# Attention scores of several heads issued in turns into one two-bank PSUM tile, value sums in two other banks

## The chip, the cores and the metric

The kernel runs on one core of a Trainium2 chip. The metric is the device time of one execution in microseconds (us), as the median of several runs. The engines are named as the profile names them: PE (TensorE, matmul), PEld (its weight loads), DVE (VectorE), ACT (ScalarE), POOL (GpSimd) and SP (SyncE, which issues the DMA transfers).

## The reference: two layers of a hybrid decoder

The input is one sequence of 256 tokens of width 1024. Each of two layers adds half a gated feed-forward block, a mixer and another half feed-forward block:

```python
for l in range(DEPTH):
    x = x + 0.5 * swiglu(rms_norm(x, norm_gain[l, 0]), w_ffn_in[l, 0], w_ffn_out[l, 0])
    x = x + hybrid_mixer(rms_norm(x, norm_gain[l, 1]), ...)
    x = x + 0.5 * swiglu(rms_norm(x, norm_gain[l, 2]), w_ffn_in[l, 1], w_ffn_out[l, 1])
```

The mixer projects its input into the queries, keys and values of four attention branches of four heads each: A (keys picked by an indexer, one shared key and value head), B (block-sparse), C (latent, with heads of 96 columns) and D (dilated, three groups of four heads, mixed by their softmax denominators). Each branch's output is projected, multiplied by a sigmoid gate, and summed over branches:

```python
branches = jnp.stack([o.reshape(b, t_len, BRANCH_WIDTH) for o in (out_a, out_b, out_c, out_d)], axis=2)
gates = jax.nn.sigmoid(gate_logits.reshape(b, t_len, N_BRANCH, D_MODEL) + b_gate)
merged = jnp.einsum('btnc,ncd->btnd', branches, w_branch)
return jnp.sum(gates * merged, axis=2) @ w_out
```

The output has the shape of the input, in float32.

## The kernel before

Tokens are handled in two tiles of 128 (`i` = 0, 1). The large products (feed-forward, projections, gates, output) run on operands that are split into a high and a low part: ACT casts a weight tile to `whi` (L187), DVE subtracts to get `wlo` (L188), and `mm3` issues three matmuls (L192 to L194). One such split serves 8 to 24 matmuls.

In the mixer the projections come first, then the attention of a branch stands beside the gates and the merge (output projection) of an earlier branch. `ORD` is B, C, A, D: the program writes the attention of B and C, then the gates and merge of B, the attention of A, gates and merge of C, the attention of D, gates and merge of A, and at last gates and merge of D. A scheduler then sets the order on each engine by priority and its own forecast of times, so that matmuls of gates and merges stand between those of the attention.

The attention of one branch and token tile (`att_tile`) loops over four heads. For each head the scores are one f32 matmul of 128 queries by n = 128 (i+1) keys (L791), for D three of them (L808 for i = 0, L817 for i = 1), one for each group. The profile shows one f32 matmul as two PE instructions. Heads of A, B and D have 64 columns, and two heads stand above each other on the partitions: even heads on rows 0 to 63, odd heads on rows 64 to 127, so that such a matmul uses one half of PE's rows. Heads of C take 96 rows. Then `softmax_pv` follows: DVE adds the bias and takes the row maximum (`tensor_tensor_reduce`, L551, called a read of the scores below), for D and i = 1 in two pieces; DVE negates it (`nm`, L557); ACT takes the exponential (L559); PE transposes the result (L567), DVE or ACT copies it (L571, L569), and PE multiplies it by the values (L574) into the tile `ov`. After four heads `finish` divides by the sums (L579, L581), transposes (L588) and splits the result (L590, L591). For A the bias is made by POOL from the indexer's choice (L799).

Eight PSUM banks are in use: two each for `pm` and `pt`, and four with the tags a0 to a3 for the rest. A score tile (`sl`) takes one bank, in turn a0, a1, a2; `ov` always takes a3:

```python
def s_tile():
    turn[0] += 1
    return pa.tile([128, 512], F32, name="sl", tag=f"a{turn[0] % 3}")[:]
```

A tile's place is given to the next tile of the same tag when all that read or wrote it have ended. The feed-forward's four sums (`acc`), the projections' pairs (`zp`) and the output's pairs (`xo`) use the same four banks.

Of the kernel before, what the change touches and what calls it, by code (L numbers as in the profile page):

```python
# [9 lines left out]
F32 = mybir.dt.float32  # L10
F32R = mybir.dt.float32r
AF = mybir.ActivationFunctionType
ALU = mybir.AluOpType
# [5 lines left out]
NT = 2  # L19
# [3 lines left out]
NFF = DFF // 128  # L23
# [4 lines left out]
CUT = -3e38  # L28
# [40 lines left out]
def tile_trunk(ctx: ExitStack, tc: tile.TileContext, a: dict, out: bass.AP):  # L69
# [145 lines left out]
    def ffn(l, s, nxt=None, aside=None):  # L215
# [86 lines left out]
        def grow(i):  # L302
            for h in range(2):
                xs = x[:, i, h * 512:(h + 1) * 512]
                nc.vector.scalar_tensor_tensor(out=xs, in0=acc[2 * i + h][:], scalar=0.5, in1=xs,
                                               op0=ALU.mult, op1=ALU.add)
                if nxt is None:
                    nc.sync.dma_start(out=out[0, i * 128:(i + 1) * 128, h * 512:(h + 1) * 512], in_=xs)
# [7 lines left out]
        def down(m, w, i):  # L316
            wh, wl = w
            ah, al = act[m]
            for h in range(2):
                t = slice(i * 128, (i + 1) * 128)  # L320
                n = slice(h * 512, (h + 1) * 512)
                mm3(acc[2 * i + h][:], ah[:, t], al[:, t], wh[:, 0, n], wl[:, 0, n], m == 0, m == NFF - 1)

        w0, todo = first(0)
        w1, more = first(1)
# [1 line left out]
        hh, hl, rs, rb, rows = yield todo  # L327
        yield from up_first(0, w0)
        rows()
        acc = [pa.tile([128, 512], F32, name=f"acc{j}", tag=f"a{j}") for j in range(4)]  # L330
        for j in range(1, NFF // 2):
            if j < 2:
                for _ in up_first(j, w1):
# [116 lines left out]
    def mixer(l, nxt):  # L450
# [6 lines left out]
            return gT[:, c:c + 1]  # L457

        def tiles():
            turn[0] += 2  # L460
            return [pa.tile([128, 512], F32, name="zp", tag=f"a{(turn[0] + i) % 4}") for i in range(NT)]

        def weights(c0, n, slots=own, pool=()):
            for q in range(2):
# [72 lines left out]

        brh, brl = {}, {}

        def softmax_pv(i, logits, pv, o, h):  # L540


            mx = sm.tile([128, 16], F32, name="mx", tag="mx")
            e = wk.tile([128, 768], F32, name="e", tag="e", bufs=3)
            off = 0
            for j, (ps, b) in enumerate(logits):
                n = int(np.prod(ps.shape[1:]))
                ev = e[:, off:off + n]
                if len(ps.shape) == 3:
                    ev = ev.rearrange("p (g s) -> p g s", g=ps.shape[1])  # L550
                nc.vector.tensor_tensor_reduce(out=ev, in0=ps, in1=b, scale=1.0, scalar=CUT, op0=ALU.add,  # L551
                                               op1=ALU.max, accum_out=mx[:, j:j + 1])
                off += n
            nm = sm.tile([128, 16], F32, name="nm", tag="nm")
            if len(logits) == 2:
# [37 lines left out]
        def pair(t, h):  # L593
            return t[64 * (h % 2):64 * (h % 2) + 64, h // 2, :]
# [191 lines left out]

        def plain(q_of, k_of, v, vh, bias_of):
            def one(i, h, o):
                n = 128 * (i + 1)
                ps = s_tile()  # L790
                nc.tensor.matmul(ps[:, :n], lhsT=q_of(h)[:, i * 128:(i + 1) * 128], rhs=k_of(h)[:, :n],  # L791
                                 start=True, stop=True)
                softmax_pv(i, [(ps[:, :n], bias_of(i, h)[:, :n])], lambda j: v[:, j, vh(h), :], o, h)
            return one

        def bias_a(i, h):
            n = 128 * (i + 1)
# [4 lines left out]
        def one_d(i, h, o):  # L802
            n = 128 * (i + 1)
            qs = slice(i * 128, (i + 1) * 128)
            if i == 0:
                ps = s_tile().rearrange("p (g s) -> p g s", g=4)
                for g in range(3):
                    nc.tensor.matmul(ps[:, g, :], lhsT=pair(dq, 4 * g + h)[:, qs], rhs=pair(dk, 4 * g + h)[:, :n],  # L808
                                     start=True, stop=True)
                bv4 = bias[:, 8:20, :].rearrange("p (g h) s -> p g h s", h=4)  # L810
                lg = [(ps[:, 0:3, :], bv4[:, :, h, 128:])]
            else:
                p0 = s_tile().rearrange("p (g s) -> p g s", g=2)
                p1 = s_tile()
                for g in range(3):
                    d = p0[:, g, :] if g < 2 else p1[:, :256]
                    nc.tensor.matmul(d, lhsT=pair(dq, 4 * g + h)[:, qs], rhs=pair(dk, 4 * g + h)[:, :n],  # L817
                                     start=True, stop=True)
                bv4 = bias[:, 8:20, :].rearrange("p (g h) s -> p g h s", h=4)
                lg = [(p0, bv4[:, 0:2, h, :]), (p1[:, :256], bias[:, 16 + h, :])]  # L820
            nb = i + 1
            softmax_pv(i, lg, lambda j: dv[:, j % nb, 4 * (j // nb) + h, :], o, h)

        one_a = plain(lambda h: pair(aq, h), lambda h: ak[64 * (h % 2):64 * (h % 2) + 64, 0, :], av,
                      lambda h: 0, bias_a)
# [1 line left out]
                      lambda i, h: bias[:, 4 + h, 256 - 128 * (i + 1):])  # L827
        one_c = plain(lambda h: cq[:, h, :], lambda h: ck[:, h, :], cv, lambda h: h,
                      lambda i, h: bias[:, 20, 256 - 128 * (i + 1):])


        yts = [wk.tile([128, 4, T], F32, name="yt", tag="xn") for _ in range(2)]
# [50 lines left out]
        for j, n in enumerate(ORD):  # L883
            for m in ORD[j + (j > 0):j + 2]:
                for i in range(NT):
                    att_tile(m, i, ones[m])
# [9 lines left out]
        def out_part(ps, i, h, e):  # L896
            t = slice(i * 128, (i + 1) * 128)
            wh, wl = w[4 * h + e]
            for k in range(2):
                kk = 2 * e + k  # L900
                mm3(ps[:], yh[kk // 4][:, kk % 4, t], yl[kk // 4][:, kk % 4, t], wh[:, k, :], wl[:, k, :],
                    kk == 0, kk == KC - 1)

        def add(ps, i, h):
            xs = x[:, i, h * 512:(h + 1) * 512]
            nc.vector.tensor_tensor(xs, ps[:], xs, op=ALU.add)

        ps = [[pa.tile([128, 512], F32, name="xo", tag=f"a{2 * h + i}") for i in range(NT)] for h in range(2)]
# [73 lines left out]
```

## Time and profile before

| | us |
|---|---|
| median of three runs | 1406.47 |
| the runs | 1399.9, 1406.47, 1406.78 |
| the profiled execution, its time | 1401.21 |
| its span, first to last instruction | 1399.4 |
| PE busy in the span | 1373.0 (98%) |
| DVE busy | 881.5 (63%) |
| ACT busy | 679.1 (49%) |
| POOL busy | 258.5 (18%) |

The profile page gives busy times of the engines, the chain of work that ended last, and the costliest groups of instructions; views of the trace list instructions in order of time with start, duration and the idle time before them. [...] The two layers stand in the trace at about 0 to 700 us and 700 to 1400 us; the attention of the first runs from 314 to 452 us, that of the second from 1003 to 1142 us.

### The profile page before, as it was taken

The numbers are of one execution on the slowest core, as the hardware profiler recorded it, in microseconds if no ns is written. First come the engines' busy times: TensorE is split into PE (matmuls) and PEld (weight loads), VectorE is DVE, ScalarE is ACT, GpSimd is POOL, SyncE is SP. The second block draws the span as 40 slices with busy tenths as digits, with TensorE's granted clock in tenths as the row PEclk, the third lists the DMA queues.
The fourth block names the chain that finished last, engine by engine and source line by source line (L and its number), as shares of the span: only waits on it lengthen the run. The fifth ranks groups of instructions, "written<-read, shape, count | busy, mean of one in ns | idle before, by whom it ended". The sixth has DMA issues, their size and how long they took to land.

```text
span 1399.4 us, 23259 instructions
## 1 busy us (share of the span) xinstructions
PE 1373.0 (98%) x9393; PEld 1262.6 (90%) x9393; DVE 881.5 (63%) x1498; ACT 679.1 (49%) x1052; POOL 258.5 (18%) x209
## 2 busy tenths in 40 slices
PE   7999999999999999999999999999999999999998
PEld 7998989879988989999999999898899989899997
DVE  6536556786696686555475555567866866765552
ACT  6425434655444556444454444355554454554441
POOL 0101132130022041111301111322200312211110
PEclk9999999999999999999999999999999999999999
DMA  9549634554442366555555555354534424665530
GB/s 353 171 158 374 239 118 127 186 167 151 127 145 77 135 206 208 189 181 181 181 170 192 181 181 196 95 185 145 188 121 148 133 70 145 214 208 193 188 121 31
DMA packets 173597, 237.10 MB, mean 169 GB/s; under 512 B 5085, under 2 KB 144545, under 8 KB 173489
## 3 DMA queue, kind: packets, MB, share of 16 engines
q1 hardware_dynamic: 172275, 235.16, 50.7%
q8 instruction: 74, 1.21, 0.3%
q10 hardware_dynamic: 1182, 0.38, 0.1%
q14 instruction: 34, 0.28, 0.1%
q0 software_dynamic: 32, 0.07, 0.0%
HBM read 234.51 MB, written 5.21 MB: 171 GB/s over the span
## 4 chain that ended last, share of the span: by engine, by line
PE 93%; DVE 3%; ACT 2%; DMA 1%; issue 1%; SPq 0%; ACTq 0%; DVEq 0%; POOLq 0%
PE pm L194 17%; PE pm L193 17%; PE pm L192 17%; PE acc L192 6%; PE acc L193 6%; PE acc L194 6%; PE zp L193 4%; PE zp L194 4%; PE zp L192 4%; PE ov L574 2%; PE sl L791 1%; DVE wlo L188 1%; PE pt L567 1%; PE xo L194 1%; PE xo L193 1%; PE sl L817 1%
## 5 line engine op out<-in xcount | busy, mean ns | idle before, releaser
L187 ACT CAST whi<-raw 128x1024 fp32r<-128x1024 f32 (+5 forms) x446 | 451.8, 1020 | 478.9 <-PE pm L193 293.1
L188 DVE TENSOR_TENSOR wlo<-raw,whi 128x1024 fp32r<-128x1024 f32 (+3 forms) x426 | 515.4, 1215 | 265.9 <-ACT whi L187 258.6
L192 PE MATMUL pm<-hh,whi 128*128 128x256 f32 x1664 | 473.8, 285 | 4.5 <-DVE tg L872 2.7
L194 PE MATMUL pm<-hh,wlo 128*128 128x256 f32 x1664 | 474.3, 285 | 0.8 <-DVE wlo L188 0.8
L193 PE MATMUL pm<-hl,whi 128*128 128x256 f32 x1664 | 473.1, 284 | 0.0
L192 PEld LDWEIGHTS pm<-hh,whi 128*128 128x128 f32 x1664 | 317.9, 191 | 9.1 <-ACT whi L187 5.0
L194 PEld LDWEIGHTS pm<-hh,wlo 128*128 128x128 f32 x1664 | 317.9, 191 | 4.7 <-issue 2.7
L193 PEld LDWEIGHTS pm<-hl,whi 128*128 128x128 f32 x1664 | 318.0, 191 | 4.4 <-issue 2.0
L296 POOL TENSOR_TENSOR act<-av,act 128x256 fp32r<-128x256 f32 x72 | 96.0, 1334 | 545.0 <-ACT act L295 540.6
L193 PE MATMUL acc<-wlo,act 128*128 128x512 f32 x352 | 138.2, 393 | 0.0
L192 PE MATMUL acc<-whi,act 128*128 128x512 f32 x352 | 138.2, 394 | 0.0
L194 PE MATMUL acc<-whi,act 128*128 128x512 f32 x352 | 137.9, 392 | 0.0
L193 PE MATMUL zp<-wlo,hh 128*128 128x512 f32 (+4 forms) x320 | 115.6, 362 | 0.2
L194 PE MATMUL zp<-whi,hl 128*128 128x512 f32 (+4 forms) x320 | 114.4, 359 | 0.0
L192 PE MATMUL zp<-whi,hh 128*128 128x512 f32 (+4 forms) x320 | 106.7, 359 | 0.0
L288 DVE TENSOR_TENSOR z<-pm,rb 128x512 f32<-128x512 f32 x72 | 49.7, 691 | 56.7 <-PE pm L194 56.5
L194 PEld LDWEIGHTS acc<-whi,act 128*128 128x128 f32 x352 | 66.1, 188 | 15.0
L192 PEld LDWEIGHTS acc<-whi,act 128*128 128x128 f32 x352 | 66.1, 188 | 13.3
L193 PEld LDWEIGHTS acc<-wlo,act 128*128 128x128 f32 x352 | 66.2, 188 | 13.1
L874 POOL TENSOR_TENSOR yt<-yt,tg 128x512 f32<-128x512 f32 x24 | 37.9, 1599 | 213.7 <-DVE tg L872 205.1
L194 PE MATMUL pm<-whi,hl 128*128 128x256 f32 x256 | 72.9, 285 | 2.6 <-DVE hl L139 2.6
L192 PE MATMUL pm<-whi,hh 128*128 128x256 f32 x256 | 73.0, 285 | 0.7 <-ACT hh L136 0.7
(191 smaller groups left out, 1794.2 us busy)
## 6 DMA issues: line engine op xcount, KB each, us to landing
raw<-in_w_ffn_in_dram SPq DMA_DIRECT2D x66, 1024.0 KB
raw<-in_w_in_dram SPq DMA_DIRECT2D x52, 1024.0 KB
raw<-in_w_ffn_out_dram SPq DMA_DIRECT2D x44, 1024.0 KB
raw<-in_w_ffn_in_dram SPq DMA_DIRECT2D x44, 512.0 KB
raw<-in_w_branch_dram SPq DMA_DIRECT2D x8, 1024.0 KB
raw<-in_w_out_dram SPq DMA_DIRECT2D x8, 1024.0 KB
raw<-in_w_in_dram SPq DMA_DIRECT2D x8, 768.0 KB
rep<-ld SPq DMA_DIRECT2D x1, 4032.0 KB
```

Of the source, the lines that this page charges most:

```text
L187: nc.scalar.copy(hv, src)
L188: (eng or nc.vector).tensor_tensor(lv, src, f(hv), op=ALU.subtract)
L192: nc.tensor.matmul(ps, lhsT=lh, rhs=rh, start=start, stop=False)
L193: nc.tensor.matmul(ps, lhsT=lh, rhs=rl, start=False, stop=False)
L194: nc.tensor.matmul(ps, lhsT=ll, rhs=rh, start=False, stop=stop)
L288: nc.vector.tensor_tensor(z[:], ps[:], rb[:].rearrange("p (o t) -> p o t", o=1) .to_broadcast([128, 2, T]), op=ALU.mult)
L296: nc.gpsimd.tensor_tensor(al, av[:], f(ah), op=ALU.subtract)
L567: nc.tensor.transpose(ps[:, c, :], p[:, (done + c) * 128:(done + c + 1) * 128], ident[:])
L574: nc.tensor.matmul(o[:, h, :], lhsT=pT[:, j, :], rhs=pv(j), start=j == 0, stop=j == nb - 1)
L791: nc.tensor.matmul(ps[:, :n], lhsT=q_of(h)[:, i * 128:(i + 1) * 128], rhs=k_of(h)[:, :n], start=True, stop=True)
L817: nc.tensor.matmul(d, lhsT=pair(dq, 4 * g + h)[:, qs], rhs=pair(dk, 4 * g + h)[:, :n], start=True, stop=True)
L874: nc.gpsimd.tensor_tensor(y, y, t[:], op=ALU.add)
```

## The change

- Scores get a tile of two banks with one tag, a01 (`s_pair`). For A, B and C the four heads of a token tile are issued one after the other, heads 0 and 2 into the first bank, 1 and 3 into the second (n columns each, at column 0 or 256). All four matmuls are written ahead of the four reads.
- For D two heads go together. For i = 0 the three groups are issued in turns (group 0 of both heads, group 1 of both, group 2 of both), one bank for each head. For i = 1 the first two groups of both heads fill one pair of banks, and group 2 of both takes a second pair.
- Two heads of a token tile share one tile `e` of exponentials where they fit (`logits_tiles`), with a maximum column of their own.
- `ov` alternates between a2 and a3.
- The feed-forward's first two sums, every second pair of projections and the first pair of the output become one tile of the tag a01 too; a2 and a3 stay single.

No instruction is added or taken away; what changes is their order and which tile a matmul waits for.

```diff
-        def s_tile():
+        def s_pair():
+
+            p = pa.tile([128, 2, 512], F32, name="sl", tag="a01")
+            return p[:, 0, :], p[:, 1, :]
+
+        def att_tile(n, i, scores, pv, together):
+
+
             turn[0] += 1
-            return pa.tile([128, 512], F32, name="sl", tag=f"a{turn[0] % 3}")[:]
-
-        def att_tile(n, i, one):
-            o = pa.tile([128, 4, 65], F32, name="ov", tag="a3")
-            for h in range(4):
-                one(i, h, o)
+            o = pa.tile([128, 4, 65], F32, name="ov", tag=f"a{2 + turn[0] % 2}")
+            for h0 in range(0, 4, together):
+                hs = range(h0, h0 + together)
+                for h, lg in zip(hs, scores(i, hs)):
+                    softmax_pv(i, lg, pv(i, h), o, h)
             finish(n, i, o)
...
+                two = s_pair()
+                ps = [two[h % 2][:, 256 * (h // 2):256 * (h // 2) + n] for h in hs]
+                for p, h in zip(ps, hs):
+                    nc.tensor.matmul(p, lhsT=q_of(h)[:, i * 128:(i + 1) * 128], rhs=k_of(h)[:, :n],
+                                     start=True, stop=True)
+                es = logits_tiles(2, n) + logits_tiles(2, n)
+                return [logits_sum(e, p, bias_of(i, h)[:, :n]) for e, p, h in zip(es, ps, hs)]
...
+            if i == 0:
+                ps = [p.rearrange("p (g s) -> p g s", g=4) for p in s_pair()]
                 for g in range(3):
...
+                    for p, h in zip(ps, hs):
+                        product(p[:, g, :], g, h)
...
+            ps = [p.rearrange("p (g s) -> p g s", g=2) for p in s_pair()]
+            for g in range(2):
+                for p, h in zip(ps, hs):
+                    product(p[:, g, :], g, h)
+            es = logits_tiles(1, 768) + logits_tiles(1, 768)
+            es = [logits_sum(e, p, bv4[:, 0:2, h, :]) for e, p, h in zip(es, ps, hs)]
+            ps = s_pair()
+            for p, h in zip(ps, hs):
+                product(p[:, :256], 2, h)
...
+        acc01 = pa.tile([128, 2, 512], F32, name="acc01", tag="a01")
+        acc = [acc01[:, 0, :], acc01[:, 1, :]]
...
+            turn[0] += 1
+            if turn[0] % 2:
+                return [pa.tile([128, 512], F32, name="zp", tag=f"a{2 + i}")[:] for i in range(NT)]
+            z = pa.tile([128, 2, 512], F32, name="zp", tag="a01")
+            return [z[:, 0, :], z[:, 1, :]]
```

**PE where the attention of D begins, first layer, before.** `sl` are scores, `pt<-ident,e` transposes of exponentials, `ov` value sums (`av_a` of branch A), `x3` three equal matmuls in a row.

```order
L567 MATMUL pt<-ident,e 128x128 x2
L808 MATMUL sl<-dk,dq 128x128 x6
L567 MATMUL pt<-ident,e 128x128 x2
L574 MATMUL ov<-av_a,pT 128x65 x2
L567 MATMUL pt<-ident,e 128x128 x2
L808 MATMUL sl<-dk,dq 128x128 x3
L574 MATMUL ov<-av_a,pT 128x65 x2
L808 MATMUL sl<-dk,dq 128x128 x3
L567 MATMUL pt<-ident,e 128x128 x2
L574 MATMUL ov<-av_a,pT 128x65 x2
L817 MATMUL sl<-dk,dq 128x256 x3
```

The same place after the change; `pm` are matmuls of gates.

```order
L830 MATMUL sl<-dk,dq 128x128 x4
L586 MATMUL ov<-av_a,pT 128x65 x2
L579 MATMUL pt<-ident,e 128x128 x2
L830 MATMUL sl<-dk,dq 128x128 x2
L192 MATMUL pm<-hh,whi 128x256
L193 MATMUL pm<-hl,whi 128x256
L194 MATMUL pm<-hh,wlo 128x256
L586 MATMUL ov<-av_a,pT 128x65 x2
L579 MATMUL pt<-ident,e 128x128 x2
L586 MATMUL ov<-av_a,pT 128x65 x2
L830 MATMUL sl<-dk,dq 128x128 x6
L586 MATMUL ov<-av_a,pT 128x65 x2
```

Before, the six scores in one row are three of head 0 and then three of head 1, and heads 2 and 3 follow alone. After, the rows of four, two and six alternate between an even and an odd head, and the next row of scores (four of 128x256, for i = 1) stands directly behind the last one above.

**DVE at the same place, before.** `ISA e,mx<-sl` is a read of scores, `ISA mx` its maximum.

```order
L571 COPY pT<-pt 128x256
L551 ISA e,mx<-sl,ba 128x256
L551 ISA mx 128x1
L188 TENSOR_TENSOR wlo<-raw,whi 128x1024
L557 TENSOR_SCALAR nm<-mx 128x1
L551 ISA e,mx<-sl,bias 128x384
L551 ISA mx 128x1
L571 COPY pT<-pt 128x256
L551 ISA e,mx<-sl,bias 128x384
L551 ISA mx 128x1
L557 TENSOR_SCALAR nm<-mx 128x1 x2
```

DVE after the change.

```order
L583 COPY pT<-pt 128x256
L558 ISA e,mx<-sl,bias 128x384
L558 ISA mx 128x1
L558 ISA e,mx<-sl,bias 128x384
L558 ISA mx 128x1
L881 TENSOR_TENSOR tg<-pm,rb 128x512
L569 TENSOR_SCALAR nm<-mx 128x1 x2
L188 TENSOR_TENSOR wlo<-raw,whi 128x1024
L558 ISA e,mx<-sl,bias 128x384
L558 ISA mx 128x1
L558 ISA e,mx<-sl,bias 128x384
L558 ISA mx 128x1
```

The reads of D's heads now come in twos, and a gate's scaling (L881) and a `wlo` stand between the reads of heads 0 and 1 and those of heads 2 and 3.

## Rows read from the trace of the kernel before

**Rows 1.** The profile page: span, busy time of engines, chain that ended last.

```profile
span 1399.4 us, 23259 instructions
PE 1373.0 (98%) x9393; PEld 1262.6 (90%) x9393; DVE 881.5 (63%) x1498; ACT 679.1 (49%) x1052; POOL 258.5 (18%) x209
PE 93%; DVE 3%; ACT 2%; DMA 1%; issue 1%; SPq 0%; ACTq 0%; DVEq 0%; POOLq 0%
```

**Rows 2.** PE in order of time, a lone 128-column score: start, duration, line, names, count.

```profile
319.79 0.28 PE L192 MATMUL pm<-hh,whi 128*128 128x256 f32 x1
320.00 0.48 PE L791 MATMUL sl<-bqk 64*128 64x128 f32 x2
320.42 0.39 PE L193 MATMUL pm<-hl,whi 128*128 128x256 f32 x1
320.64 0.28 PE L194 MATMUL pm<-hh,wlo 128*128 128x256 f32 x1
320.76 0.27 PE L192 MATMUL pm<-hh,whi 128*128 128x256 f32 x1
```

**Rows 3.** PE in order of time: one 128-column score of branch C.

```profile
332.29 0.37 PE L193 MATMUL pm<-hl,whi 128*128 128x256 f32 x1
332.49 0.38 PE L791 MATMUL sl<-ck,cq 96*128 96x128 f32 x2
332.63 0.36 PE L194 MATMUL pm<-hh,wlo 128*128 128x256 f32 x1
332.83 0.28 PE L192 MATMUL pm<-hh,whi 128*128 128x256 f32 x1
```

**Rows 4.** PE in order of time: a lone 256-column score; then a row of two.

```profile
411.56 0.28 PE L193 MATMUL pm<-hl,whi 128*128 128x256 f32 x1
411.77 0.70 PE L791 MATMUL sl<-aqk 64*128 64x256 f32 x2
412.39 0.39 PE L194 MATMUL pm<-hh,wlo 128*128 128x256 f32 x1
412.62 0.28 PE L192 MATMUL pm<-hh,whi 128*128 128x256 f32 x1
...
325.53 0.28 PE L194 MATMUL pm<-hh,wlo 128*128 128x256 f32 x1
325.74 0.70 PE L791 MATMUL sl<-bqk 64*128 64x256 f32 x4
326.37 0.39 PE L192 MATMUL pm<-hh,whi 128*128 128x256 f32 x1
326.59 0.28 PE L193 MATMUL pm<-hl,whi 128*128 128x256 f32 x1
```

**Rows 5.** PE in order of time: scores of branch D.

```profile
429.37 1.26 PE L808 MATMUL sl<-dk,dq 64*128 64x128 f32 x12
431.55 0.93 PE L808 MATMUL sl<-dk,dq 64*128 64x128 f32 x6
434.62 1.56 PE L817 MATMUL sl<-dk,dq 64*128 64x256 f32 x6
449.29 1.13 PE L817 MATMUL sl<-dk,dq 64*128 64x256 f32 x4
```

**Rows 6.** DVE and PE in order of time where D begins.

```profile
430.54 1.22 DVE L188 TENSOR_TENSOR wlo<-raw,whi 128x1024 fp32r<-128x1024 f32 x1
431.68 0.15 DVE L557 TENSOR_SCALAR nm<-mx 128x1 f32<-128x1 f32 x1
431.74 0.55 DVE L551 CUSTOM_DVE_ANT_1 e<-sl,bias 128x384 f32<-128x384 f32 x1
432.21 0.42 DVE L571 COPY pT<-pt 128x256 f32<-128x256 f32 x1
...
429.26 0.69 DVE L849 TENSOR_TENSOR tg<-pm,rb 128x512 f32<-128x512 f32 x1 [0.23 <-PE pm L194]
437.51 0.44 PE L588 MATMUL pt<-ident,bo 128*128 128x128 f32 x2 [0.73 <-DVE bo L581]
```

**Rows 7.** Busy us (and instructions) by stretch; then granted clock, DMA share and rate.

```profile
385.00:420.00 35.00, 33.67 (x248) 30.07 (x247) 31.35 (x88) 16.41 (x28) 9.05 (x8) 1.00 0.45 143
420.00:455.00 35.00, 34.12 (x242) 29.29 (x241) 23.61 (x67) 16.31 (x28) 7.98 (x9) 1.00 0.24 79
1110.00:1145.00 35.00, 34.11 (x243) 29.29 (x242) 23.61 (x68) 16.23 (x27) 8.42 (x8) 1.00 0.26 85
```

More of the change, by code (lines that the diff above doesn't have):

```diff
@@ L304, in grow @@
                 xs = x[:, i, h * 512:(h + 1) * 512]
-                nc.vector.scalar_tensor_tensor(out=xs, in0=acc[2 * i + h][:], scalar=0.5, in1=xs,
+                nc.vector.scalar_tensor_tensor(out=xs, in0=acc[2 * i + h], scalar=0.5, in1=xs,
                                                op0=ALU.mult, op1=ALU.add)
@@ L329, in ffn @@
         rows()
-        acc = [pa.tile([128, 512], F32, name=f"acc{j}", tag=f"a{j}") for j in range(4)]
+        acc01 = pa.tile([128, 2, 512], F32, name="acc01", tag="a01")
+        acc = [acc01[:, 0, :], acc01[:, 1, :]]
+        acc += [pa.tile([128, 512], F32, name=f"acc{j}", tag=f"a{j}")[:] for j in (2, 3)]
         for j in range(1, NFF // 2):
@@ L538, in mixer, with logits_tiles, logits_sum @@
         brh, brl = {}, {}
-        def softmax_pv(i, logits, pv, o, h):
[L543 to L553, printed above, removed]
+        def logits_tiles(n, ncol):
+            e = wk.tile([128, 768], F32, name="e", tag="e", bufs=3)
+            return [(e[:, j * ncol:(j + 1) * ncol], 0, sm.tile([128, 16], F32, name="mx", tag="mx"), 0)
+                    for j in range(n)]
+        def logits_sum(e, ps, b):
+            ev, off, mx, j = e
+            n = int(np.prod(ps.shape[1:]))
+            out = ev[:, off:off + n]
+            if len(ps.shape) == 3:
+                out = out.rearrange("p (g s) -> p g s", g=ps.shape[1])
+            nc.vector.tensor_tensor_reduce(out=out, in0=ps, in1=b, scale=1.0, scalar=CUT, op0=ALU.add,
+                                           op1=ALU.max, accum_out=mx[:, j:j + 1])
+            return ev, off + n, mx, j + 1
+        def softmax_pv(i, logits, pv, o, h):
+            e, off, mx, parts = logits
             nm = sm.tile([128, 16], F32, name="nm", tag="nm")
-            if len(logits) == 2:
+            if parts == 2:
                 nc.vector.tensor_tensor(mx[:, 0:1], mx[:, 0:1], mx[:, 1:2], op=ALU.max)
@@ L774, in mixer, with scores @@
         project(4036, 256, lambda i, ps: values(i, ps, 0, 4, dv, 8))
-        def s_tile():
+        def s_pair():
+            p = pa.tile([128, 2, 512], F32, name="sl", tag="a01")
+            return p[:, 0, :], p[:, 1, :]
+        def att_tile(n, i, scores, pv, together):
             turn[0] += 1
-            return pa.tile([128, 512], F32, name="sl", tag=f"a{turn[0] % 3}")[:]
-        def att_tile(n, i, one):
-            o = pa.tile([128, 4, 65], F32, name="ov", tag="a3")
-            for h in range(4):
-                one(i, h, o)
+            o = pa.tile([128, 4, 65], F32, name="ov", tag=f"a{2 + turn[0] % 2}")
[3 more added lines that the diff above has]
+                    softmax_pv(i, lg, pv(i, h), o, h)
             finish(n, i, o)
         def plain(q_of, k_of, v, vh, bias_of):
-            def one(i, h, o):
+            def scores(i, hs):
                 n = 128 * (i + 1)
[L790 to L794, printed above, removed]
+                two = s_pair()
[5 more added lines that the diff above has]
+                return [logits_sum(e, p, bias_of(i, h)[:, :n]) for e, p, h in zip(es, ps, hs)]
+            return scores, lambda i, h: lambda j: v[:, j, vh(h), :], 4
         def bias_a(i, h):
@@ L800, in bias_a, with scores_d, product @@
             return b
-        def one_d(i, h, o):
+        bv4 = bias[:, 8:20, :].rearrange("p (g h) s -> p g h s", h=4)
+        def scores_d(i, hs):
             n = 128 * (i + 1)
             qs = slice(i * 128, (i + 1) * 128)
+            def product(d, g, h):
+                nc.tensor.matmul(d, lhsT=pair(dq, 4 * g + h)[:, qs], rhs=pair(dk, 4 * g + h)[:, :n],
+                                 start=True, stop=True)
             if i == 0:
-                ps = s_tile().rearrange("p (g s) -> p g s", g=4)
+                ps = [p.rearrange("p (g s) -> p g s", g=4) for p in s_pair()]
@@ L807, in one_d @@
                 for g in range(3):
[L808 to L820, printed above, removed]
+                    for p, h in zip(ps, hs):
+                        product(p[:, g, :], g, h)
@@ new lines, in scores_d @@
+                es = logits_tiles(2, 384)
+                return [logits_sum(e, p[:, 0:3, :], bv4[:, :, h, 128:]) for e, p, h in zip(es, ps, hs)]
+            ps = [p.rearrange("p (g s) -> p g s", g=2) for p in s_pair()]
[5 more added lines that the diff above has]
+            ps = s_pair()
@@ L829, in mixer @@
                       lambda i, h: bias[:, 20, 256 - 128 * (i + 1):])
+        one_d = scores_d, pv_d, 2
         yts = [wk.tile([128, 4, T], F32, name="yt", tag="xn") for _ in range(2)]
@@ L885, in mixer @@
                 for i in range(NT):
-                    att_tile(m, i, ones[m])
+                    att_tile(m, i, *ones[m])
             tg = iter(list(gates(n, indexer() if j == 0 else ())))
@@ L905, in add @@
             xs = x[:, i, h * 512:(h + 1) * 512]
-            nc.vector.tensor_tensor(xs, ps[:], xs, op=ALU.add)
-        ps = [[pa.tile([128, 512], F32, name="xo", tag=f"a{2 * h + i}") for i in range(NT)] for h in range(2)]
+            nc.vector.tensor_tensor(xs, ps, xs, op=ALU.add)
+        xo = pa.tile([128, 2, 512], F32, name="xo", tag="a01")
+        ps = [[xo[:, 0, :], xo[:, 1, :]],
+              [pa.tile([128, 512], F32, name="xo", tag=f"a{2 + i}")[:] for i in range(NT)]]
         for h in range(2):
```

10 lines of the change are left out of this document (5 added, 5 removed).

## The prediction

> **What bounds the kernel now.** I read the page first: PE is busy 98% of the span, and the chain that ended last runs 93% on PE, 3% on DVE [rows 1]. So PE's time is the kernel's time wherever PE does not wait, and a change pays by what it takes from PE's row of starts. Next I read the timeline of PE around the scores. Two neighbouring gate matmuls start 0.12 us apart (320.64 and 320.76). Where a lone score of 128 columns stands between them, the matmul before it starts at 319.79 and the second one behind it at 320.64: 0.85 us where two steps of 0.12 would do, so the score takes 0.61 us [rows 2]. A score of branch C has the same columns but 96 rows, and takes 332.83 - 332.29 - 0.24 = 0.30 us [rows 3]. The score on one half of PE's rows thus costs 0.31 us more than its own work, and the starts show where: 0.21 from the gate matmul to the score and 0.39 instead of 0.28 for the matmul behind it. I call this a **break**: one for each unbroken row of half-row scores, however long.
>
> A lone 256-column score takes 412.62 - 411.56 - 0.24 = 0.82 us. Two such scores in a row, of an even and an odd head, also take 326.59 - 325.53 - 0.24 = 0.82 us: four instructions last 0.70 us, as two do [rows 4]. So two heads on different halves run side by side. In branch D three 128-column scores of one head last 0.93 us, three and three of two heads 1.26, not twice 0.93; on one half, two 256-column scores last 1.13 and three 1.56 [rows 5]. Rows 2 and 4 give the rule: a row of scores costs its duration plus 0.12 us; one more score on the same half adds 0.22 us (128 columns) or 0.43 us (256 columns), one on the other half nothing.
>
> **Scores, step by step, one layer.** Before, 23 rows of half-row scores stand in PE's order. B: four lone ones of 128, a pair and two lone ones of 256: 4 x 0.61 + 3 x 0.82 = 4.9 us. A: three lone ones of 128, a pair of 128 and 256 columns (as the pair of rows 4, 0.82), three lone ones of 256: 1.8 + 4 x 0.82 = 5.1. D: 1.26 + 0.12, twice 0.93 + 0.12, and twice each 1.56, 1.13 and 0.70 (+ 0.12 each): 11.0. Sum 21.0 us.
>
> After, the order has 13 rows, alternating between halves. B and A each: four of 128 (two on each half, 0.61 + 0.22 = 0.83), three of 256 (two on one half, 1.25) and one of 256 (0.82): 2.9. The fourth is split off, so it pays its own break. D: four, two and six of 128 (two, one, three on a half: 0.83 + 0.61 + 1.05) and twice each four and two of 256 (1.25, 0.82): 6.6. Sum 12.4 us. Saved: 8.6 us a layer, of which ten breaks fewer are 3.1 and the overlap of the halves 5.5. The second layer shows the same work at the same place (DVE 23.61 us in both stretches, [rows 7]), so 17.2 us in all. C's matmuls break nothing and gain nothing.
>
> **Waits that are added.** Before, three banks rotate: a score waits for one read, three heads back. After, the next tile of scores waits until all reads of the last one have ended; queued behind it on PE are the transposes and gate matmuls, and casts and `wlo` wait for those in turn. Eleven such hand-overs come in a layer. At nine of them the order puts 23 or more other matmuls between, at least 23 x 0.12 = 2.8 us, against up to four reads (0.47 each, from a 384-column read at 431.74 to the next DVE start at 432.21) and a `wlo` of 1.22 [rows 6]: about 3.1. I take these as covered; uncovered they cost 0.3 or more each.
>
> Two have next to nothing between them, both where D begins. From D's first two heads to the other two there are nine matmuls, some 1.2 us with the break, against a copy of 0.42 and two reads of 0.47 plus their ends, some 1.5: PE loses 0.3. From there to D's second token tile only two matmuls stand on PE. DVE still has a scaling of 0.69, two `nm` of 0.15, a `wlo` of 1.22 and two reads, 3.2 us after it released PE; PE spends 1.27 on six scores and two value sums: it loses about 2.0. Before, PE waited 0.73 us for `bo` there [rows 6]; now four scores of 1.25 us hide `bo`. Net 1.5 us a layer; bounds 0 (the DVE work is done early) and 3.
>
> Two smaller terms. Between 385 and 420 us DVE is busy 31.35 of 35 us with the indexer [rows 7]: what PE arrives earlier may be given back there. And the order shifts transposes of the projections forward by up to some twenty matmuls, towards the results that they wait for. Bounds for both together: 0 and 4 us a layer (DVE's idle 3.65 us in that stretch); I take 1.0, near the low end, as PE is busy 33.67 of the 35 us there today. The second bank for `ov` I cost at nothing: PE waits for no `ov` bank today, so there is nothing to win. Feed-forward and output keep their order but for a few neighbours: nothing.
>
> **The sum.** 8.6 - 1.5 - 1.0 = 6.1 us a layer, 12.2 in all, on the profiled 1401.21: 1389.0. That execution lies 5.3 us below the median 1406.47, and the three runs fall on both (1399.9, and 1406.47 with 1406.78); I add half of it: **1391.6**.
>
> **Rivals.**
> *The halves overlap only in part.* Then a score on the other half starts beside the second instruction of the one before it, not beside its first. For it: in the row of twelve [rows 5] the second head cost 0.33, not nothing. Against it: the pair in rows 4, where 0.70 would have been 0.91. The price is 0.21 for each of six rows of 256 and 0.11 for each of five of 128 columns, 1.8 us a layer: 1395.2. [...]
> *Not at all side by side.* Only breaks are saved, and scores on the other half cost as on the same one: 18.1 us a layer after, 2.9 saved, 2.5 given to waits: 1403. The pair of rows 4 speaks against it.
> *DVE takes it all back.* The reads come in clumps of two and four, a `wlo` behind them is up to 2 us later, and each of the eleven hand-overs costs PE 0.8 us: 8.6 + 8.8 would cancel, about 1404. For it: the hand-over worked out above at 2.0, and a DVE at 90% in the indexer's stretch. Against it: 23 matmuls or more at nine places, and DVE at 67% where D stands [rows 7].
> *Slower.* The same hand-overs, each waiting for its reads and a `wlo` that went first: 4 x 0.47 + 1.22 against a cover of 1.6, 1.5 us each, 16.5 a layer: +7.9 a layer, 1420. It decides from 1.1 us a hand-over on (0.8 that cancel, and 0.3 to leave the band). Against it: the nine covered places.
>
> **How the numbers follow.** The forecast has 0.62, part overlap 0.08, no overlap 0.04, all taken back 0.18, slower 0.08. The range reaches from all 17.2 us at the lower of the two levels (1384) up to the case in which DVE takes it back: 1383 to 1405. About 0.5%, 7 us, is what a measurement of this kernel can tell from no change. Forecast and part overlap lie beyond it on the faster side: 0.70. No overlap and taken back lie within: 0.22. Slower: 0.08.
>
> **What would show it.** In the changed kernel's timeline a row of four 128-column scores should last 0.70 us where a lone one lasts 0.48, and four of 256 columns in two halves 1.13. The 46 rows of half-row scores should be 26, and their cost 25 us, not 42. PE should wait some 2 us for a read of scores where D's second token tile begins, in both layers. The prediction is wrong if rows of four last as long as four scores on one half (128 columns: 1.15), or if waits of PE for reads of scores sum to over 9 us a layer.

## The result, and the profile after

The changed kernel takes 1394.37 us (median of seven runs, 1391.08 to 1396.54) against 1406.47: a ratio of 0.9926, with an interval of 0.9911 to 0.9941. That is faster, by 8 to 12.5 us. The profiled execution took 1394.26 us.

The page of the changed kernel, as in [rows 1]: span, busy time (share) and instructions of the engines, and the chain that ended last.

```profile
span 1392.5 us, 23262 instructions
PE 1358.7 (98%) x9393; PEld 1254.2 (90%) x9393; DVE 875.7 (63%) x1498; ACT 676.4 (49%) x1052; POOL 265.0 (19%) x209
PE 91%; DVE 5%; ACT 2%; issue 1%; DMA 1%; POOL 0%; SPq 0%; ACTq 0%; DVEq 0%; POOLq 0%
```

PE is busy for 14.3 us less with the same instructions, and the span is only 6.9 us shorter: PE waits more, and DVE's share of the chain rose from 3 to 5%. The lengths of the stages on PE say where. They are worked out from the starts of its instructions: from the first to the last matmul of the projections (`zp`), from there to the first of the output (`xo`; attention, gates and merges), in us; the kernels below "after" are experiments.

```
            before zp   zp 1st layer   attention 1st   zp 2nd   attention 2nd   span
before        207.4        110.0          174.0         110.1       173.7      1399.4
after         206.2        113.1          167.8         113.1       167.8      1392.5
split         208.6        109.5          169.0         109.5       169.9      1390.7
major         207.8        113.1          166.7         113.1       168.1      1393.4
ov1           207.7        114.0          167.7         113.1       167.8      1394.9
pairs         207.4        114.6          181.9         113.7       183.4      1425.6
glue          207.4        109.5          165.8         109.5       167.3      1383.7
full          207.6        109.7          166.8         109.8       166.5      1384.5
gluefull      208.4        109.5          169.3         109.6       167.8      1388.8
index         207.5        109.5          164.6         109.6       163.1      1378.4
```

The change wins 6.2 and 5.9 us in the two attentions and loses 3.1 and 3.0 us in the two projections. The feed-forward in between and at the end moved by 0.2 us each. Ahead of the projections runs differ by 2 us with the clock: from 100 to 150 us its granted share was 1.00 in the changed kernel, 0.97 in the kernel before and 0.93 in split.

PE in order of time after the change (start, duration, line, names, count, and in brackets the idle time ahead and what ended it): the rows that answer to [rows 2] and [rows 4].

```profile
323.64 0.28 PE L194 MATMUL pm<-hh,wlo 128*128 128x256 f32 x1
323.85 0.71 PE L811 MATMUL sl<-bqk 64*128 64x128 f32 x8
324.50 0.39 PE L192 MATMUL pm<-hh,whi 128*128 128x256 f32 x1
324.72 0.28 PE L193 MATMUL pm<-hl,whi 128*128 128x256 f32 x1
324.84 0.28 PE L194 MATMUL pm<-hh,wlo 128*128 128x256 f32 x1
...
328.53 1.13 PE L811 MATMUL sl<-bqk 64*128 64x256 f32 x6
329.58 0.44 PE L579 MATMUL pt<-ident,e 128*128 128x128 f32 x2
329.95 0.70 PE L811 MATMUL sl<-bqk 64*128 64x256 f32 x2
```

Neighbouring gate matmuls start 0.12 us apart here (324.72 and 324.84) and are listed with 0.28 us each, so costs are read from starts. Four scores of 128 columns (eight PE instructions) last 0.71 us and cost 324.72 - 323.64 - 0.24 = 0.84; one alone cost 0.61 [rows 2]. The fourth score of 256 columns is split off by two transposes, as its order had shown. Over both layers the 46 rows of half-row scores became 26. Their cost, summed in the same way, fell from 41.7 to 26.9 us, 2.05 of it a wait: 24.9 without.

The waits of PE in the changed kernel (who waits, for whom, us in total, times, longest).

```profile
PE pt L513 <- DVE zn L526: 3.4, 4, 1.2
PE pt L600 <- DVE bo L593: 2.1, 2, 1.0
PE sl L830 <- DVE nm L569: 2.1, 2, 1.0
PE ov L586 <- DVE pT L583: 1.4, 2, 0.7
PE pt L513 <- DVE zn L622: 1.2, 2, 0.6
PE zp L192 <- ACT whi L187: 1.2, 2, 0.6
PE zp L193 <- DVE wlo L188: 1.1, 2, 0.5
```

The four lines with `zn` or `zp` lie in the projections and did not exist before: 6.9 us, of which 0.9 stand for a wait that is gone there. The whole view sums to 29.4 us, before to 21.7.

Windows of the changed kernel (busy us and instructions of PE, PEld, DVE, ACT and POOL; granted clock, DMA share, GB/s).

```profile
352.00:356.00 4.00, 2.25 (x18) 1.81 (x17) 3.72 (x10) 3.16 (x7) 0.11 (x1) 1.00 0.27 112
356.00:360.00 4.00, 4.00 (x24) 4.00 (x24) 1.11 (x6) 1.01 (x3) 0.00 (x0) 0.57 0.02 4
1042.00:1046.00 4.00, 4.00 (x24) 4.00 (x23) 1.55 (x8) 0.99 (x3) 0.00 (x0) 0.57 0.01 4
```

In each layer the granted clock is 0.57 over 4 us, and 0.50 in each microsecond from 357 to 359 and from 1043 to 1045 us; in the first, PE had just stood idle for 1.75 of 4 us. Gate matmuls start 0.21 us apart in the first of the two (357.11 and 357.32) instead of 0.12. I estimate the price of a stretch from its granted share, 0.43 x 4 = 1.7 us; the fifteen steps from 356.06 to 359.24 us give some 1.4 (3.18 us for 1.8). Before, no such stretch lay in the attention: the granted clock was 1.00 from 314 to 460 us and from 1003 to 1145 us.

### The profile page after: what moved, and what is told of

It is laid out like the page before. It is cut to its first block, busy times and chain, and to the rows that moved or that the text cites. A ratio compares the mean times of both kernels' runs of the same rounds, so it can differ in the third digit from the quotient of the medians.

```text
span 1392.5 us, 23262 instructions
## 1 busy us (share of the span) xinstructions
PE 1358.7 (98%) x9393; PEld 1254.2 (90%) x9393; DVE 875.7 (63%) x1498; ACT 676.4 (49%) x1052; POOL 265.0 (19%) x209
## 4 chain that ended last, share of the span: by engine, by line
PE 91%; DVE 5%; ACT 2%; issue 1%; DMA 1%; POOL 0%; SPq 0%; ACTq 0%; DVEq 0%; POOLq 0%
PE pm L192 17%; PE pm L194 17%; PE pm L193 17%; PE acc L192 6%; PE acc L193 6%; PE acc L194 6%; PE zp L193 4%; PE zp L194 4%; PE zp L192 4%; PE ov L586 2%; DVE wlo L188 2%; PE pt L579 1%; PE sl L811 1%; PE xo L194 1%; PE xo L193 1%
## 5 line engine op out<-in xcount | busy, mean ns | idle before, releaser
L192 PE MATMUL zp<-whi,hh 128*128 128x512 f32 (+4 forms) x320 | 110.1, 361 | 1.2 <-ACT whi L187 1.2
L906 POOL TENSOR_TENSOR yt<-yt,tg 128x512 f32<-128x512 f32 x24 | 40.9, 1725 | 204.7 <-DVE tg L904 198.0
L114 POOL TENSOR_TENSOR rs<-ms,neg_half 128x4 f32<-128x4 f32 (+3 forms) x44 | 53.5, 1223 | 124.9 <-DVE ms L111 124.9
```

Source lines behind the costliest of these rows:

```text
L114: nc.gpsimd.tensor_tensor(rs[:, :n], ms[:, :n], neg_half[:, :n], op=ALU.pow)
L906: nc.gpsimd.tensor_tensor(y, y, t[:], op=ALU.add)
```

## Experiments

**1. Single tiles for projections and scores (split).** The heads still go in turns, but every bank has a tag of its own again.

```diff
-            p = pa.tile([128, 2, 512], F32, name="sl", tag="a01")
-            return p[:, 0, :], p[:, 1, :]
+            return [pa.tile([128, 512], F32, name="sl", tag=f"a{j}")[:] for j in range(2)]
...
-            turn[0] += 1
-            if turn[0] % 2:
-                return [pa.tile([128, 512], F32, name="zp", tag=f"a{2 + i}")[:] for i in range(NT)]
-            z = pa.tile([128, 2, 512], F32, name="zp", tag="a01")
-            return [z[:, 0, :], z[:, 1, :]]
+            turn[0] += 2
+            return [pa.tile([128, 512], F32, name="zp", tag=f"a{(turn[0] + i) % 4}")[:] for i in range(NT)]
```

> The changed kernel with its order of issue kept (heads in turns, four scores of A, B and C ahead of their reads), but the two banks of scores are two tiles with a tag of their own (a0, a1), and the pairs of the projections, of the first feed-forward sums and of the output are single tiles that rotate over a0 to a3 as before. Theory (the two-bank tiles hold the projections up): the waits of PE in the projections, which rose from 2.4 us before to 8.4 us after in both layers together, fall back to about 2.4, the cost of the scores stays at about 25 us, and the time is about 6 us below the changed kernel (some 1388). Rival (the order of the attention moves the projections' transposes, whatever the tiles are): the waits in the projections stay at 8 us and the time stays within 2 us of the changed kernel (1394).

Measured: 1392.72 us (1391.65 to 1392.98). The waits in the projections are gone to the last line; what is left in one layer's (205 to 312 us of split):

```profile
PE pm L193 <- DVE wlo L188: 0.8, 1, 0.8
PE pm L192 <- DVE rs L116: 0.4, 1, 0.4
```

Both lines stand in the kernel before too. So the two-bank tiles cause the added waits, not the order of the attention. The time did not follow, since I had overlooked the other end: with a tag for each bank the scheduler issues a score as soon as its own bank is free, the rows fall apart again (35 instead of 26), and the scores cost 34.5 us. The projections got 3.6 us shorter in each layer, the attention 1.2 and 2.1 longer. The time missed the expected 1388 by nearly 5 us.

**2. The two-bank tiles alone (pairs).** The kernel before, with the projections' pairs in two-bank tiles; its scores, issued head by head, then have two banks to rotate over instead of three.

```diff
-            return pa.tile([128, 512], F32, name="sl", tag=f"a{turn[0] % 3}")[:]
+            if turn[0] % 2:
+                return pa.tile([128, 512], F32, name="sl", tag="a2")[:]
+            return pa.tile([128, 2, 512], F32, name="sl", tag="a01")[:, 0, :]
```

> The kernel before with single issue of scores, but its projections' pairs, first feed-forward sums and first output pair are two-bank tiles as in the changed kernel; scores rotate between one bank of the two-bank tag and a2, ov stays in a3. Theory (two-bank tiles hold the projections up): the waits of PE in the projections are some 6 us above the 2.4 us of before, the cost of the scores stays at 42 us, and the time is some 6 us above before (1406 to 1412, the one bank fewer for scores may add some). Rival (the attention's order moves the transposes): waits in the projections stay at 2.4 us and the time stays at that of before within 2 us, but for waits of scores for their bank.

Measured: 1426.38 us, a ratio of 1.0161 (1.0142 to 1.0181) to the kernel before: slower by 22 us. The waits of the projections appear, line by line those of the changed kernel:

```profile
PE sl L798 <- DVE mx L556: 3.5, 4, 0.9
PE pt L513 <- DVE zn L526: 3.3, 4, 1.2
...
PE pt L513 <- DVE zn L615: 1.2, 2, 0.6
...
PE zp L193 <- DVE wlo L188: 1.0, 2, 0.5
...
PE zp L192 <- ACT whi L187: 0.9, 2, 0.6
```

That confirms the first point, but the time that I expected for the run (1406 to 1412) was far off. The rest goes with the missing bank for scores: PE waits four times for a read of scores, and windows around D show what follows:

```profile
425.00:435.00 10.00, 8.30 (x62) 7.33 (x62) 8.68 (x23) 5.32 (x10) 2.96 (x3) 1.00 0.52 173
435.00:455.00 20.00, 19.95 (x86) 16.61 (x87) 7.81 (x29) 5.49 (x12) 1.11 (x4) 0.57 0.04 17
...
1135.00:1158.00 23.00, 22.14 (x91) 18.01 (x90) 8.96 (x33) 6.36 (x14) 2.83 (x3) 0.55 0.09 37
```

After 1.7 us of idle time in ten, PE is granted 0.57 of its clock over 20 us, and 0.55 over 23 us in the second layer (0.50 in each microsecond from 437 to 453 and from 1137 to 1156 us). From these shares I estimate 0.43 x 20 = 8.6 and 0.45 x 23 = 10.4 us, enough for the 7.9 and 9.7 us that the two attentions lost, and several times the waits themselves. Whether the waits brought the lower clock about, no run shows.

**3. One head, then the other, inside a row (major).**

```diff
-                for p, h in zip(ps, hs):
+                for h in (0, 2, 1, 3):
+                    p = ps[h]
...
-                for g in range(3):
-                    for p, h in zip(ps, hs):
+                for p, h in zip(ps, hs):
+                    for g in range(3):
```

> The changed kernel, but inside each row of scores all instructions of the even half come before those of the odd half (A, B and C: heads 0, 2, 1, 3; D: all groups of one head, then those of the other). Number of rows, tiles and reads stay. Theory (heads overlap because neighbours in the order use different halves): rows of four lose their overlap but for the one neighbouring pair in the middle; a row of four of 128 columns takes about 0.9 us instead of 0.70, four of 256 about 1.5 instead of 1.13, and the time rises by about 3 us a layer, 6 in all (some 1400). Rival (the order inside a row does not matter, only that it is one row): row durations as in the changed kernel, time within 2 us of it.

Measured: 1395.96 us (1395.22 to 1397.34); scores 27.8 us instead of 26.9 (26.4 and 24.9 without their waits). The rival is nearer to it, but not for every row. A row of four of B, and D's row of six, in the order of time:

```profile
325.50 0.72 PE L812 MATMUL sl<-bqk 64*128 64x128 f32 x8
...
433.16 1.26 PE L831 MATMUL sl<-dk,dq 64*128 64x128 f32 x12
```

Four PE instructions of the even half ahead of four of the odd half take 0.72 us, as in turns (0.71); four of one half alone last 0.71 (D's two scores of one head at 430.96 us of this run), so the odd half adds 0.01. Six ahead of six take 1.26 instead of 0.94. Why the order counts for six and not for four, no run shows, and none tried other numbers. The turns gain only in D; what counts for A and B is that four scores stand in one row.

**4. One bank for the value sums (ov1).**

```diff
-            o = pa.tile([128, 4, 65], F32, name="ov", tag=f"a{2 + turn[0] % 2}")
+            o = pa.tile([128, 4, 65], F32, name="ov", tag="a3")
```

> The changed kernel with all value sums in one bank (a3) again, as before. Theory (the second bank is worth nothing): time within 1 us of the changed kernel (1393 to 1396) and no wait of PE for an ov bank. Rival (with the scores of four heads issued together the sums of the next token tile come closer, and the second bank is needed): PE waits at the first value sum of a token tile for the read of bo, 0.3 us or more at each of 16 places, 5 us or more in all.

Measured: 1395.42 us (1392.65 to 1396.85). At a mean clock of 0.998 its runs took 1393.94 and 1394.22 and those of the changed kernel 1394.26 and 1394.37, and its attentions are as long. No wait for an `ov` bank appeared. The second bank is worth nothing.

**5. Single tiles, and rows kept whole (glue).** Run 1 with one edge more in the order: `held` is the last read of the row before, and the first score of a row waits for it.

```diff
+        def row(ins):
+            for r in held:
+                tc.add_manual_dep(ins, r.name,
+                                  mybir.DependencyInfo(mybir.DependencyClass.Sync, mybir.DependencyReason.DATA),
+                                  reason="row")
+            held.clear()
...
                     nc.tensor.matmul(p, lhsT=q_of(h)[:, i * 128:(i + 1) * 128], rhs=k_of(h)[:, :n],
                                      start=True, stop=True)
+                    row(nc.cur_bb.bb.instructions[-1])
```

> Single-bank tiles everywhere, as in the run split, and one ordering edge more: the first score of a row waits for the last read of the row of scores before it (for the first row: the last read of the projections), so that a row is not pulled apart when one bank comes free before the other. Theory (two-bank tiles cost 6 us in the projections, and what split lost again was the pulling apart of rows): the scores cost 23 to 25 us as in the changed kernel, less 1.5 where A's four scores of 256 columns now stand in one row, the waits in the projections are 2.4 us, and the time is some 7 us below the changed kernel, 1385 to 1388. Rival (a row that waits for both banks gives the gain of split back as waits of PE for reads of scores): waits for reads of scores of 4 us or more, time within 2 us of split (1392.7).

Measured: 1385.54 us (1384.13 to 1386.21), a ratio of 0.9867 (0.9847 to 0.9887) to the kernel before. 24 rows, 24.1 us; the projections are as short as in split. A's four scores of 256 columns, two rows in the changed kernel, are one:

```profile
410.62 1.13 PE L815 MATMUL sl<-aqk 64*128 64x256 f32 x8
411.69 0.39 PE L193 MATMUL pm<-hl,whi 128*128 128x256 f32 x1
```

The one line of its waits that names a score:

```profile
PE sl L835 <- DVE mx L555: 0.5, 2, 0.3
```

Waiting for both banks costs 0.5 us in all, not 4. The rival falls, and the change's own gain is there without the loss in the projections.

**6. All rows of PE for each score (full).** The kernel before, with `pair` (one half) replaced by `both`.

```diff
+        def both(t, h):
+            return t[:, h // 2, :]
...
-        one_b = plain(lambda h: pair(bq, h), lambda h: pair(bk, h), bv, lambda h: h,
+        one_b = plain(lambda h: both(bq, h), lambda h: both(bk, h), bv, lambda h: h,
```

> The kernel before, but each score of A, B and D takes all 128 rows of PE instead of one half (so it sums the products of two heads and the output is another one; the number, columns and order of the instructions stay). Theory (what a row of half-row scores pays beside its own columns is a fixed 0.31 us for going to half rows and back): a lone 128-column score takes 0.30 us or less instead of 0.61, a lone 256-column score some 0.5 instead of 0.82; the 46 rows save 14 us, of which 1 to 2 are lost where two halves overlapped (pair of 256 columns, row of twelve): scores 28 to 30 us instead of 41.7, time 12 to 13 us below the kernel before (at a clock of 0.999: 1388 to 1390). Rival (the price belongs to f32 scores as such, not to half rows): a lone score takes 0.61 us still and the time stays that of before, or rises by the overlap lost.

Measured: 1386.34 us (1386.25 to 1387.67), 14.9 us less span than before. The lone scores of [rows 2] and [rows 4] with full rows:

```profile
319.58 0.28 PE L192 MATMUL pm<-hh,whi 128*128 128x256 f32 x1
319.70 0.39 PE L794 MATMUL sl<-bqk 128*128 128x128 f32 x2
319.84 0.36 PE L193 MATMUL pm<-hl,whi 128*128 128x256 f32 x1
320.04 0.28 PE L194 MATMUL pm<-hh,wlo 128*128 128x256 f32 x1
...
408.18 0.28 PE L193 MATMUL pm<-hl,whi 128*128 128x256 f32 x1
408.29 0.60 PE L794 MATMUL sl<-aqk 128*128 128x256 f32 x2
408.54 0.47 PE L194 MATMUL pm<-hh,wlo 128*128 128x256 f32 x1
408.84 0.28 PE L192 MATMUL pm<-hh,whi 128*128 128x256 f32 x1
```

320.04 - 319.58 - 0.24 = 0.22 us instead of 0.61, and 408.84 - 408.18 - 0.24 = 0.42 instead of 0.82. The price of going to half rows is 0.39 us for the one and 0.40 for the other. All 46 rows cost 26.7 us instead of 41.7, less than the 28 to 30 expected. The two attentions are 14.4 us shorter, the span 14.9.

**7. All rows of PE, and rows kept whole (gluefull).** The edit of run 6 on run 5.

> The run glue, with all 128 rows of PE for each score of A, B and D (the output is another one). Theory (a row of scores in turns gains one fixed price of 0.31 us less and the overlap of two halves more): without halves there is neither; a row of four of 128 columns takes about 0.9 us as before, one of four of 256 columns 1.75 instead of 1.26, six of 128 columns 1.3 instead of 1.0; in all 3.5 to 5 us slower than glue, and within 2 us of the run full, since without halves it does not matter how scores are grouped. Rival (grouping helps by itself, whatever the rows): gluefull is faster than full by more than 4 us and as fast as glue.

Measured: 1388.11 us (1386.70 to 1390.62), 2.6 above glue and 1.8 above full. Scores 27.7 us: 3.6 above glue, 1.0 above full. A's four scores of 256 columns:

```profile
412.98 1.89 PE L818 MATMUL sl<-aqk 128*128 128x256 f32 x8
```

With full rows grouping brought nothing (27.7 us for the scores in rows of four, 26.7 in full). The theory holds; in the medians the distance to glue is smaller than the 3.5 to 5 us expected, in the summed cost of the scores it is 3.6. Between the shorter attentions of the two (glue's first, 165.8 us, and gluefull's second, 167.8) it is 2.0 us; twice that, 4.0, is my estimate for both layers.

**8. The indexer's scores on all rows (index).** Run 5, and the price of part rows taken out at another place: sixteen lone matmuls on 32 rows.

```diff
-            transposed(iq, zi, i, 1)
+            zt = pt.tile([128, 4, 128], F32, name="pt", tag="pt")
+            nc.tensor.transpose(zt[:, 0, :], zi[:, 0:128], ident[:])
+            for h in range(4):
+                hp = slice(32 * h, 32 * h + 32)
+                nc.scalar.copy(iqs[h][hp, i * 128:(i + 1) * 128], zt[hp, 0, :])
...
-                    nc.tensor.matmul(ps[:, :n], lhsT=iq[hp, 0, i * 128:(i + 1) * 128], rhs=ik[hp, 0, :n],
-                                     start=True, stop=True, tile_position=(32 * h, 0))
+                    nc.tensor.matmul(ps[:, :n], lhsT=iqs[h][:, i * 128:(i + 1) * 128], rhs=ik[:, 0, :n],
+                                     start=True, stop=True)
```

> The run glue, and in addition the indexer's scores (four heads of 32 rows each, 16 lone matmuls in both layers, two PE instructions each) take all 128 rows of PE: ACT copies each head's queries into a tile of its own in which the other rows are zero, four copies of 32 rows for one of 128, and POOL clears three tiles more a layer. Theory (a matmul on part of the rows between full ones pays a fixed price, 0.37 to 0.39 us by the run full, whatever it computes and however many rows it uses): the sixteen cost some 5.2 us (8 x 0.22 and 8 x 0.43, the prices of full-row scores in the run full) instead of 12.2, and the time is about 7 us below glue, 1377 to 1380. Rival (the indexer's stretch is bound by DVE and ACT, which stand beside PE there with 31 of 35 us busy, so what PE saves is given back as waits): waits of PE grow by 4 us or more and the time stays within 3 us of glue (1385.5).

Measured: 1380.21 us (1377.17 to 1381.45), a ratio of 0.9825 (0.9803 to 0.9847): the fastest of all, 23 us below the kernel before. PE at the first index score, of glue and then of this run:

```profile
376.59 0.38 PE L598 MATMUL pt<-ident,bo 128*128 128x128 f32 x2
376.90 0.48 PE L659 MATMUL pt<-ik,aqk 32*128 32x128 f32 x2
377.31 0.38 PE L192 MATMUL pm<-hh,whi 128*128 128x256 f32 x1
377.53 0.28 PE L193 MATMUL pm<-hl,whi 128*128 128x256 f32 x1
```

```profile
378.18 0.38 PE L598 MATMUL pt<-ident,bo 128*128 128x128 f32 x2
378.39 0.39 PE L667 MATMUL pt<-ik,aqk 128*128 128x128 f32 x2
378.54 0.36 PE L192 MATMUL pm<-hh,whi 128*128 128x256 f32 x1
378.74 0.28 PE L193 MATMUL pm<-hl,whi 128*128 128x256 f32 x1
```

From the first transpose to the second gate matmul 0.94 us became 0.56. The sixteen cost 5.6 us instead of 12.2, and the medians differ by 5.3: 0.8 us more of waits for `tg` take part of the rest. DVE gave no more back than that, so the rival falls; the 7 us expected were not reached.

## Why the prediction was right, and where it was off

**Direction and mechanism: right.** PE's row of starts set the end, and the scores gave what they were said to give. Predicted 26 rows and 25 us, a row of four of 128 columns at 0.70 us and four of 256 in two halves at 1.13; measured 26 rows, 24.9 us without the wait, 0.71 and 1.13. Saved 16.8 us, predicted 17.2. The forecast of 1391.6 us is 2.8 below the median; part of that closeness is luck, as the sum below shows.

**The price of a break was too small**, 0.31 for 0.39 us (run 6). I took branch C's score as one without a break; its own cost is 0.30, a full-row score's 0.22. The sum did not suffer, because it was made from measured rows of before; only the split of the 8.6 us was off, 3.9 for breaks and 4.7 for the overlap by the same ten breaks.

**The term that failed: the projections.** I let the transposes that move forward there and the indexer's stretch cost 1.0 us a layer together, near the low end of 0 to 4, because PE was busy 33.67 of 35 us in the indexer's stretch. That row spoke of the wrong stage. The projections alone lost 3.0 us a layer, and runs 1 and 2 show the cause, the two-bank tile: by the program's rule it comes free only when the reads of both token tiles have ended. No run changed `zp` alone, but no score stands in the projections before their end. The trace suggests how the tile acts: two transposes of `zn`, and the next pair behind them, wait for the second token tile's `zn`, which ends at 237.51 us. Before, that `zn` was done at 233.80 us and its transposes stood at 240.40, behind the first matmuls of that pair (238.11).

```profile
237.66 0.41 PE L513 MATMUL pt<-ident,zn 128*128 128x128 f32 x2 [0.62 <-DVE zn L622]
```

The edit that looked like bookkeeping (one tile for two banks in `zp`) was the dearest part of the change.

**The hand-overs: right in kind.** Ten of eleven in a layer are covered, as assumed of nine. Where D's second token tile begins, PE waits, in both layers; PE and DVE there:

```profile
432.60 0.94 PE L830 MATMUL sl<-dk,dq 64*128 64x128 f32 x12
432.83 1.22 DVE L188 TENSOR_TENSOR wlo<-raw,whi 128x1024 fp32r<-128x1024 f32 x1
433.46 0.66 PE L586 MATMUL ov<-av_a,pT 128*128 128x65 f32 x4
...
434.44 0.55 DVE L558 CUSTOM_DVE_ANT_1 e<-sl,bias 128x384 f32<-128x384 f32 x1
...
435.15 1.13 PE L830 MATMUL sl<-dk,dq 64*128 64x256 f32 x8 [1.02 <-DVE nm L569]
```

It waits 1.02 us, not 2.0. DVE does what I listed (scaling, `wlo`, two reads) from 432.11 to 435.0, 2.9 us for my 3.2; but PE comes to the six scores only at 432.60, half a microsecond after the release, and spends 1.5 us on them and the four value sums, not 1.27. At the second pair it doesn't wait at all (0.3 predicted): PE comes to its six scores only at 432.60 us, after DVE's reads of the first pair (the last begins at 431.63 and takes 0.55). In all, the attention's waits rose by 0.7 us a layer (from 2.7 to 3.4, before and after, 314 to 460 us) where I had a net 1.5: the 0.73 for `bo` [rows 6] is covered there, as said, but a wait of 1.0 for another `bo` came at 353 us.

**A term that was missing: the clock.** In the changed kernel's profile, idle PE time at that `bo` and the value sums behind it (1.03 and 0.72 us in each layer) is followed by a stretch at the lower clock, 1.7 us each by the estimate above (1.4 by the starts). The attention's account then closes: 8.4 saved, 0.7 and 1.7 given back, 6.0 left (6.3 with 1.4); measured 6.2 and 5.9. That the idle time brings the lower clock about, no run shows. In glue (run 5) PE stands idle equally long at this place in both layers (1.78 us of 8), and the stretch follows in the second alone (windows in the columns used above):

```profile
349.00:357.00 8.00, 6.22 (x55) 5.62 (x53) 5.83 (x19) 5.05 (x11) 0.11 (x1) 1.00 0.22 89
1030.00:1038.00 8.00, 6.22 (x40) 5.87 (x39) 4.99 (x18) 4.08 (x9) 0.00 (x0) 0.79 0.17 67
```

Its attentions took 165.8 and 167.3 us. Major has the stretch in the second layer alone (0.50 from 1042 to 1045 us), and its attention is 1.4 us longer there; ov1 has it in both (0.50 from 359 to 361 and from 1045 to 1047 us), split in neither. In gluefull and index the attentions of the two layers differ by 1.5 us. What decides whether the stretch comes, no run shows.

**The sum.** Predicted 6.1 us a layer, 12.2 in all. Measured between the profiled executions 6.9: two attentions of 6.0, less two projections of 3.0, and 0.9 that other stages differ by. The 0.9 is mainly the clock ahead of the projections (1.2), less 0.4 lost in the feed-forward. The medians differ by 12.1 only because the profiled execution of before was one of its faster ones; the interval allows 8 to 12.5. At a mean granted clock of 1.000 the kernel before took 1399.90 us (an execution taken beside runs 1 to 4) and the changed kernel 1391.08 and 1391.12: 8.8 us apart. The terms without the clock give nearly the same: 2 x (8.4 - 0.7 - 3.0) - 0.4 = 9.0. That the medians lie as far apart as the sum said is therefore luck; at an equal clock the change wins about three quarters of it.

**The rivals.** Partial overlap would have shown in the rows of four; they last what full overlap gives (0.71 and 1.13 us, for 0.70 and 1.13 predicted). Run 3 speaks against it too: four instructions of the odd half behind four of the even one end within 0.72 us, when four alone last 0.71. Not at all side by side falls with the same rows. DVE takes all back: waits for reads of scores are 2.1 us over both layers, against 0.8 at each of eleven places; what was given back went another way. Slower: the change pays for one hand-over a layer. Run 2 did become slower with waits for reads of scores, but only 3.5 us of them; most of its loss is the projections and, by the estimate there, the clock.

Runs 6 and 8 give the price of a lone matmul on part of the rows: 0.39 us for a score of 128 columns on half of them (0.61 less 0.22), 0.38 for the first index score, on 32 (0.94 less 0.56).

## What to carry to other kernels

In this kernel a matmul on part of PE's rows between full ones cost 0.38 to 0.40 us more than on all rows, and rows of four were cheaper than lone ones (26 rows for 24.9 us, 46 for 41.7). Where a trace shows the same, try to put such matmuls in one row, with the halves side by side, or to give them all rows with zeros where that needs little extra work (run 8: 5.3 us). Tie the row together by an edge in the order, not by a larger tile: a tile over two banks can delay all who use the same banks for something else (here the projections, by 3.0 us a layer). Before calling a change of tiles neutral, look at every stage that takes tiles of that tag, not at the stage that the change is for.

## Not expected of the hardware

- Four instructions of one half of PE's rows ahead of four of the other last no longer than the eight in turns (0.72 and 0.71 us), but six ahead of six do (1.26 instead of 0.94 us).
- A lone full-row score was cheaper than a lone half-row one: 0.22 and 0.61 us (128 columns), 0.42 and 0.82 us (256 columns). In rows of four the half-row scores were (24.1 against 27.7 us for all scores).
- In run 2 the lower clock cost more, by the estimate there (8.6 and 10.4 us), than the waits ahead of it: 0.57 for 20 us and 0.55 for 23 us behind waits of under 2 us in ten. In glue PE was idle for 1.78 of 8 us in both layers, and the lower clock followed in one of them. The changed kernel's runs follow the mean clock: they took 1391.1 us at 1.000, 1394.3 at 0.998 and 1396.5 at 0.995.
